# Backward queries kept in natural time order, and the two normed scan directions added on GpSimd, in a hybrid RWKV-7 / gMLP layer

## The chip, the cores and the metric

The kernel runs on one core of one Trainium2 chip. The metric is the time of one execution in microseconds of device time. Before the change it is 3197.58 us, the median of 3 runs (3194.99 to 3198.23).

## The reference, cut to what matters

One layer is computed over 640 tokens: 512 latent tokens (a grid of 64 columns) and 128 context tokens. Half of the mixing width goes through a bidirectional RWKV-7 scan with 16 heads of 64 channels, and it is the output of that scan that the change touches.

```python
def _delta_scan(r, w, k, v, aa, bb, s0, reverse):
    ...
    def step(S, inp):
        r_t, w_t, k_t, v_t, a_t, b_t = inp
        sa = jnp.einsum('bhvk,bhk->bhv', S, a_t)
        S = S * w_t[:, :, None, :] + sa[..., None] * b_t[:, :, None, :] + v_t[..., None] * k_t[:, :, None, :]
        return S, jnp.einsum('bhvk,bhk->bhv', S, r_t)
    s_fin, ys = lax.scan(step, s0, xs, reverse=reverse)
    return jnp.moveaxis(ys, 0, 1), s_fin

def _rwkv7_bidir(p, s0, lp):
    ...
    for d in range(2):
        ...
        y, s_fin = _delta_scan(rh, decay, kd, vh, -kk, kk * heads(a),
                               s0[:, d].astype(F32), reverse=(d == 1))
        out = out + _group_norm(y, lp['gn_w'], lp['gn_b']) \
            + jnp.sum(rh * kd * lp['r_k'], axis=-1, keepdims=True) * vh
        finals.append(s_fin)
    o = (out.reshape(B, T, D_A) * gate).astype(dtype)
```

The group norm runs over the 64 channels of a head, for each token and each direction by itself; the normed outputs of both directions are then added token by token. The rest of the layer (a gMLP half, the output projection, a SwiGLU block and RMS norms) is not touched.

## The kernel before, in words

All matrices are kept with channels on the partitions and the 640 tokens along the free axis. A *pair* is two heads, that is 128 channels; there are eight pairs. A *chunk* is 64 tokens; there are ten, eight latent and two context.

**First stage: per-pair preparation.** `take_k` (line 810) builds, for each pair and each direction `d`, a tile `R` with two halves per chunk: half 0 holds the scaled removal keys and half 1 the scaled queries (line 880). For the backward direction (`d == 1`) time runs backward inside a chunk; the helper `rev` (line 840) writes both halves with the 64 positions of a chunk reversed. `tail` (line 918) multiplies `X` and `R` chunk by chunk on TensorE into `pG`, and VectorE cuts the result with a triangular mask: columns 64 to 127, the query columns, go to `GR` (line 936). `R`, `GR` and the other factors are stored in the record `d_S` in device memory. The order of all instructions in this stage is planned by `Lister` (line 248), a planner that emits each instruction by a cost worked out from shapes alone (`Op`, line 104).

**Second stage: the recurrence.** `recur(p)` (line 1406) takes the chunks of a pair in order, both directions together. Its products on TensorE are `w_ps` (L1461), `u_ps` (L1476), `s_ps` (L1497) and the outputs `y_ps` (L1427, L1432), each with small steps on VectorE and ScalarE in between. ScalarE copies the outputs into `u.Y` (L1446), with tokens of a chunk on the partitions: 64 positions of head 0, then 64 positions of head 1, and channels along the free axis. For the backward direction the positions stand in reverse.

**The finish of a pair.** `finish(p)` (line 1511) normalises `u.Y` for each direction. GpSimd subtracts the mean (L1526), ScalarE squares (L1530), VectorE sums (L1531), GpSimd takes the inverse root (the helper `rsqrt`, L386) and multiplies by it (L1536), in two halves of five chunks each. TensorE then turns the result to channels on partitions and adds both directions on the way: for each chunk and head one product with the identity `I2` for the forward direction, and one with the reversed identity `J2` (line 1354) for the backward one, which undoes the reversal; both accumulate in the same PSUM tile `pO` (L1544). VectorE scales that into `bv` (L1548), the gate follows (`pG2`, L1562, L1563), and the result is stored to `d_o` (L1566).

```python
            for (a, b) in hv:
                ps = po.tile([P, 5, CH], F32, tag="g", name="pO")
                for cc in range(a, b):
                    for h in range(2):
                        for d in range(2):
                            TE.matmul(ps[hsl(h), cc - a, :], u.Y[hsl(h), d, cc, :], (J2 if d else I2)[hsl(h), :],
                                      start=(d == 0), stop=(d == 1))
```

**What orders the second stage.** A loop over hops (line 1603) advances up to two pairs of `recur`, and runs two mixers: `m2` holds the `finish` of the pair before, `m3` holds filler work, the part of the output projection that does not depend on the scan (`wout`, L1329 to L1331, and the turning of the input `pxT`, L1587). A mixer takes steps by a budget written into the `yield` statements. The engines' order within this stage is then set by the scheduler of the framework, from the program order and its own estimates; each engine's queue is fixed when the program is built, and an engine waits in order. After the loop, `finish` of the last pair runs with what is left of the filler work (lines 1617 to 1621), and the third stage, the other half of the output projection (L1736 to L1738), reads `d_o` back.

Of the kernel before, what the change touches and what calls it, by code (L numbers as in the profile page):

```python
# [10 lines left out]
F32 = mybir.dt.float32  # L11
# [3 lines left out]
ALU = mybir.AluOpType  # L15
# [4 lines left out]
P = 128  # L20
# [5 lines left out]
CH = 64  # L26
# [309 lines left out]
def flow_step(ctx: ExitStack, tc, x_prompt, x_sample, state_rwkv, c, c_ctx, w_mod, b_mod,  # L336
# [4 lines left out]
    V, S, G, TE = nc.vector, nc.scalar, nc.gpsimd, nc.tensor  # L341
# [21 lines left out]
    I2 = cb.tile([P, CH], F32, name="I2")  # L363
# [97 lines left out]
    with ExitStack() as ph:  # L461
# [38 lines left out]
        for t in range(NT):  # L500
            xt, c1 = xall[:, t, :], slice(t, t + 1)
# [139 lines left out]
    v3 = lambda ap: ap.rearrange("p (c t) -> p c t", t=CH)  # L641
# [7 lines left out]
    hsl = lambda h: slice(64 * h, 64 * h + 64)  # L649
# [160 lines left out]
    def take_k(pr, p, read):  # L810
# [28 lines left out]
        for d in range(2):  # L839
            rev = (lambda ap: ap[:, :, ::-1]) if d else (lambda ap: ap)  # L840
            last = 0 if d else CH - 1

            sg = bk.tile([P, T], F32, tag="t1", name="sg", bufs=2)
            tha = bp.tile([P, T], F32, tag="t3", name="tha", bufs=1)
            for hf in range(2):
                s = slice(HALF * hf, HALF * hf + HALF)
                for h, dst in enumerate((sg, tha)):
                    yield slots.free
                    ps = slots.tile([P, HALF], F32, "pwa")
                    yield lambda: (p, d) in wl  # L850
                    yield [oT.matmul(ps, w[:, h, :], waM[:, h, s], start=i == 0, stop=i == 1) for i, w in enumerate(wl[p, d])]
                    c = 16 * h + 8 * d + p
                    yield oS.activation(dst[:, s], ps, AF.Tanh, scale=0.5, bias=w0h[:, c:c + 1])
                    slots.done(ps)
            del wl[p, d]
            yield oS.activation(sg, sg, AF.Copy, scale=0.5, bias=0.5)
            L = bp.tile([P, T], F32, tag="t2", name="L", bufs=1)
            for lo in (0, HALF):
                s = slice(lo, lo + HALF)
                o_, i_ = (L[:, s][:, ::-1], sg[:, s][:, ::-1]) if d else (L[:, s], sg[:, s])  # L860
                yield oV.tensor_tensor_scan(out=o_, data0=scan1, data1=i_, initial=0.0, op0=ALU.mult, op1=ALU.add)
            gam = bk.tile([P, T], F32, tag="t1", name="gam", bufs=2)
            yield oS.activation(gam, L, AF.Exp, scale=-KAP)
            yield oS.activation(L, L, AF.Exp, scale=KAP)
            yield oS.copy(gend[:, p, d, :], v3(gam)[:, :, last])
            n3, g3, i3 = v3(nkk), v3(gam), v3(L)
            n = 2 * p + d
            yield lambda: gone["R"] == n
            R = bz.tile([P, NCH, 2, CH], F32, tag="R", name="R")
            ra = rev(R[:, :, 0, :])  # L870
            if d:
                yield oV.tensor_mul(ra[:, :, 0:CH - 1], n3[:, :, 0:CH - 1], g3[:, :, 1:CH])
                yield oS.copy(ra[:, :, CH - 1], n3[:, :, CH - 1])
            else:
                yield oV.tensor_mul(ra[:, :, 1:CH], n3[:, :, 1:CH], g3[:, :, 0:CH - 1])
                yield oS.copy(ra[:, :, 0], n3[:, :, 0])
            f = fs if d == 0 else bk.tile([P, T], F32, tag="t1", name="f", bufs=2)
            yield oS.activation(f, tha, AF.Identity, scale=kah[:, p:p + 1], bias=ka1[:, p:p + 1])
            zr = o.zr
            yield oV.tensor_mul(rev(R[:, :, 1, :]), v3(zr), g3)  # L880
            yield oQ.dma_start(d_S[p, :, d, :, F_R:F_R + P], R.rearrange("p c s t -> p c (s t)"))
            yield oV.scalar_tensor_tensor(out=tha, in0=tha, scalar=1.0, in1=nkk, op0=ALU.add, op1=ALU.mult)
            yield oV.tensor_mul(f, f, zk)

            yield lambda: gone["X"] == n
            X = bz.tile([P, NCH, 2, CH], F32, tag="X", name="X", bufs=1)
            yield oV.scalar_tensor_tensor(out=rev(X[:, :, 1, :]), in0=v3(tha), scalar=-0.5, in1=i3, op0=ALU.mult, op1=ALU.mult)
            yield oV.tensor_mul(rev(X[:, :, 0, :]), v3(f), i3)
            qT.append(tail(p, d, R, X))
            if d:  # L890
                yield oV.tensor_add(fs, fs, f)
# [26 lines left out]
    def tail(p, d, R, X):  # L918
# [6 lines left out]
        for (c0, c1) in ((0, 4), (4, 8), (8, NCH)):  # L925
            yield slots.pair
            two = [slots.tile([P, 4, P], F32, "pG") for h in range(2)]
            yield [oT.matmul(two[h][(osl if u else hsl)(h), cc - c0, :], X[hsl(h), cc, u, :],
                            R[hsl(h), cc, :, :].rearrange("p s t -> p (s t)"), start=True, stop=True)
                   for cc in range(c0, c1) for u in range(2) for h in (1, 0)]  # L930
            for h in range(2):
                s, q, ps = hsl(h), osl(h), two[h]
                mb = mask.unsqueeze(1).to_broadcast([P, c1 - c0, P])
                yield oS.copy(GB[q, c0:c1, :], ps[q, 0:c1 - c0, 0:CH])
                GR = bk.tile([P, 4, CH], F32, tag="GR", name="GR", bufs=2)
                yield oV.tensor_tensor(out=GR[:, 0:c1 - c0, :], in0=ps[:, 0:c1 - c0, CH:P], in1=mb[:, :, CH:P], op=ALU.mult)
                yield oV.tensor_tensor(out=GA[s, c0:c1, :], in0=ps[s, 0:c1 - c0, 0:CH], in1=mb[s, :, 0:CH], op=ALU.mult)
                slots.done(ps)
                yield oQ.dma_start(d_S[p, :, d, c0:c1, F_G + CH * h:F_G + CH * h + CH], GR[:, 0:c1 - c0, :])
# [405 lines left out]
    with ExitStack() as ph:  # L1345
# [4 lines left out]
        po = ph.enter_context(tc.tile_pool(name="po", bufs=1, space=PSUM))  # L1350
        py = ph.enter_context(tc.tile_pool(name="py", bufs=1, space=PSUM))

        J2 = sm.tile([P, CH], F32, name="J2", bufs=1)
        V.tensor_copy(J2, I2[:, ::-1])
        gh, gl, gq = (rw.tile([P, T], F32R, name=n) for n in ("gh", "gl", "gq"))
        nc.sync.dma_start(gl.bitcast(F32), d_gs[0:P])
        S.copy(gh, gl.bitcast(F32))
# [153 lines left out]
        def finish(p):  # L1511
# [9 lines left out]
            u = U[p]  # L1521
            for d in range(2):
# [11 lines left out]
                rsqrt(ys, ys)  # L1534
                for (a, b) in hv:
                    GNE.tensor_tensor(out=y[:, a:b], in0=y[:, a:b], in1=bc(ys[:, a:b], b - a), op=ALU.mult)  # L1536
                yield 2.0

            for (a, b) in hv:
                ps = po.tile([P, 5, CH], F32, tag="g", name="pO")  # L1540
                for cc in range(a, b):
                    for h in range(2):
                        for d in range(2):
                            TE.matmul(ps[hsl(h), cc - a, :], u.Y[hsl(h), d, cc, :], (J2 if d else I2)[hsl(h), :],  # L1544
                                      start=(d == 0), stop=(d == 1))
                    yield 0.4
                dst = v3(bv)[:, a:b, :]
                V.scalar_tensor_tensor(out=dst, in0=ps, scalar=prm[:, C_GW + p:C_GW + p + 1],  # L1548
                                       in1=dst, op0=ALU.mult, op1=ALU.add)
                yield 0.8  # L1550
# [736 lines left out]
```

## Time and profile before

| what | us |
|---|---|
| median of 3 runs | 3197.58 |
| the profiled execution: its own time | 3198.94 |
| its span, first to last instruction | 3197.2 |
| TensorE busy (matmul) | 3091.0 |
| VectorE busy | 2333.2 |
| ScalarE busy | 1450.4 |
| GpSimd busy | 1276.2 |
| first and last product into `pO` (L1544), from the start of the span | 1104.9 and 1336.7 |

Times in a timeline are counted from the start of the span. The recurrence and the finishes lie between about 1045 and 1341 us. A product of 32-bit operands appears in the trace as two matmul records and two weight loads, so the 320 products of L1544 (eight pairs, ten chunks, two heads, two directions) are 640 records. "64\*64" in a record means that the product uses a 64 by 64 part of the array, so that products of the two heads can run side by side. A matmul's own duration is longer than its share of the engine, because matmuls are pipelined: the spacing of starts says what one costs. "Idle before" names the idle time of an engine in front of an instruction, and what ended it.

### The profile page before, as it was taken

The page shows a single profiled execution, that of the slowest core. Times are in us where ns is not written, and L with a number is a line of the kernel's source. Part 1 is how long each engine was busy: PE and PEld are TensorE (multiplying, and loading weights), DVE is VectorE, ACT ScalarE, POOL GpSimd, SP SyncE. Part 2 cuts the span into 40 slices and gives each one's busy share as a digit, 9 for nine tenths or more (in the row PEclk, how much of TensorE's full clock was granted, in tenths as well). Part 3 has the DMA queues.
Part 4 walks back from the last instruction along what each step waited for, and adds up shares of the span by engine and source line. Part 5 has one row for each costly group of instructions (what it writes and reads, how often), then busy time and mean ns, then how long its engine had stood idle before and what let it go on. Part 6 is the DMA issues. An engine that isn't in the chain of part 4 may idle for free.

```text
span 3197.2 us, 73695 instructions
## 1 busy us (share of the span) xinstructions
PE 3091.0 (97%) x28892; PEld 2876.7 (90%) x28892; DVE 2333.2 (73%) x4104; ACT 1450.4 (45%) x3173; POOL 1276.2 (40%) x1138
## 2 busy tenths in 40 slices
PE   7999999999998999999899999999999999999996
PEld 4888888888878777889899999999999999999996
DVE  4567687776656667567887887877878777877787
ACT  4244555555533433246444444444444444444365
POOL 1001232322221132220456665666666644555543
PEclk9999999999999999999999999999999999999998
DMA  9768988889896677356343434334433354554453
GB/s 343 239 186 245 239 228 220 219 232 234 237 235 202 206 226 240 109 153 183 109 127 107 122 118 126 119 108 129 125 111 119 111 183 147 168 162 134 121 172 122
DMA packets 742331, 552.98 MB, mean 173 GB/s; under 512 B 142112, under 2 KB 678720, under 8 KB 733152
## 3 DMA queue, kind: packets, MB, share of 16 engines
q1 hardware_dynamic: 727280, 529.73, 56.1%
q0 software_dynamic: 12288, 17.95, 2.4%
q8 instruction: 227, 3.72, 0.5%
q14 instruction: 120, 0.98, 0.1%
q10 hardware_dynamic: 2416, 0.60, 0.1%
HBM read 438.74 MB, written 111.69 MB: 172 GB/s over the span
## 4 chain that ended last, share of the span: by engine, by line
PE 85%; DMA 5%; issue 4%; DVE 4%; ACT 1%; POOL 1%; SPq 0%; DVEq 0%; ACTq 0%; POOLq 0%
PE big L106 16%; PE P L1899 15%; PE P L1897 15%; PE P L1898 15%; DMA wt<-in_w_mod_dram 2%; PE pmod L106 2%; PE big L1329 2%; PE pG L106 1%; PE pblk L106 1%; PE big L1330 1%; PE big L1331 1%; PE y_ps L1432 1%; PE u_ps L1476 1%; DMA opd<-d_op 1%; DVE lo L1687 1%
## 5 line engine op out<-in xcount | busy, mean ns | idle before, releaser
L1899 PE MATMUL P<-xo,lo 128*128 128x320 f32 x2352 | 727.8, 310 | 7.4 <-DVE lo L1687 7.4
L1897 PE MATMUL P<-xo,hi 128*128 128x320 f32 x2352 | 728.0, 310 | 2.2 <-ACT hi L1686 2.2
L1898 PE MATMUL P<-xo,hi 128*128 128x320 f32 x2352 | 727.7, 309 | 0.0
L1687 DVE TENSOR_TENSOR lo<-raw,hi 128x512 fp32r<-128x512 f32 x532 | 517.2, 979 | 163.4 <-ACT hi L1686 161.3
L1686 ACT CAST hi<-raw 128x512 fp32r<-128x512 f32 x532 | 330.4, 622 | 505.4 <-PE P L1898 425.7
L1899 PEld LDWEIGHTS P<-xo,lo 128*128 128x128 f32 x2352 | 442.4, 188 | 7.9 <-DVE lo L1687 7.9
L1897 PEld LDWEIGHTS P<-xo,hi 128*128 128x128 f32 x2352 | 442.6, 188 | 2.4 <-ACT hi L1686 2.4
L1898 PEld LDWEIGHTS P<-xo,hi 128*128 128x128 f32 x2352 | 442.6, 188 | 0.0
L1797 POOL TENSOR_TENSOR raw<-raw 128x512 f32<-128x512 f32 x252 | 412.8, 1641 | 17.3 <-DVE lo L1687 4.1
L1897 PE MATMUL P<-xd,hi 128*128 128x320 f32 x1232 | 383.0, 311 | 7.2 <-ACT hi L1686 3.4
L106 PE MATMUL big<-h_hi,hi 128*128 128x320 f32 x1184 | 388.4, 328 | 0.7 <-DVE early L600 0.7
L1899 PE MATMUL P<-xd,lo 128*128 128x320 f32 x1232 | 383.2, 311 | 3.7 <-DVE lo L1687 3.6
L1898 PE MATMUL P<-xd,hi 128*128 128x320 f32 x1232 | 382.3, 310 | 0.1
L106 PE MATMUL big<-h_hi,lo 128*128 128x320 f32 x1184 | 365.2, 308 | 0.3 <-DVE lo L106 0.3
L106 PE MATMUL big<-h_lo,hi 128*128 128x320 f32 x1184 | 365.3, 308 | 0.0
L1797 POOL TENSOR_TENSOR t<-raw 128x512 f32<-128x512 f32 x84 | 133.3, 1587 | 460.5 <-DMA raw<-in_w_ffn_up_dram 348.2
L1686 ACT CAST hi<-rawd 128x512 fp32r<-128x512 f32 (+1 forms) x288 | 165.6, 585 | 225.6 <-PE P L1898 152.1
L106 PEld LDWEIGHTS big<-h_hi,hi 128*128 128x128 f32 x1184 | 223.3, 189 | 33.9 <-issue 28.8
L1687 DVE TENSOR_TENSOR lo<-rawd,hi 128x512 fp32r<-128x512 f32 (+1 forms) x288 | 218.8, 767 | 43.0 <-ACT hi L1686 39.3
L1897 PEld LDWEIGHTS P<-xd,hi 128*128 128x128 f32 x1232 | 232.7, 189 | 10.1 <-ACT P L2195 5.1
L1899 PEld LDWEIGHTS P<-xd,lo 128*128 128x128 f32 x1232 | 232.5, 189 | 6.2 <-DVE lo L1687 6.1
L1898 PEld LDWEIGHTS P<-xd,hi 128*128 128x128 f32 x1232 | 232.6, 189 | 0.5 <-DVE xd L1950 0.5
(408 smaller groups left out, 6423.5 us busy)
## 6 DMA issues: line engine op xcount, KB each, us to landing
wt<-in_w_mod_dram SPq DMA_DIRECT2D x96, 1024.0 KB
raw<-in_w_ffn_gate_dram SPq DMA_DIRECT2D x182, 256.0 KB
raw<-in_w_ffn_up_dram SPq DMA_DIRECT2D x182, 256.0 KB
rec<-d_S SPq DMA_DIRECT2D x80, 576.0 KB
raw<-in_w_in_dram SPq DMA_DIRECT2D x166, 256.0 KB
rawd<-in_w_ffn_down_dram SPq DMA_DIRECT2D x128, 256.0 KB
raw<-in_w_out_dram SPq DMA_DIRECT2D x96, 256.0 KB
xd<-d_os SPq DMA_DIRECT2D x66, 320.0 KB
```

Source lines behind the costliest of these rows:

```text
L106: self.eng, self.run = eng, lambda: fn(*args, **kw)
L1329: TE.matmul(halves[hf], hi[:, k, :], o_hi[kb][:, s], start=(k == 0), stop=False)
L1330: TE.matmul(halves[hf], hi[:, k, :], o_lo[kb][:, s], start=False, stop=False)
L1331: TE.matmul(halves[hf], lo[:, k, :], o_hi[kb][:, s], start=False, stop=(k == 3))
L1432: TE.matmul(ys[d][hsl(h), e, :], r[:, d, F_G + CH * h:F_G + CH * h + CH], r[:, d, F_Z + CH * h:F_Z + CH * h + CH], **kw)
L1476: TE.matmul(ups[q, d, :], r[q, d, F_T:F_T + CH], r[q, d, F_Z + CH * h:F_Z + CH * h + CH] if W is None else W[q, d, :], start=True, stop=True)
L1686: S.copy(hi[:, 0:nk], raw[:, 0:nk])
L1687: V.tensor_sub(lo[:, 0:nk], raw[:, 0:nk], hi[:, 0:nk].bitcast(F32))
L1797: G.tensor_tensor(out=o[:, 0:nk], in0=p[:, 0:nk], in1=q[:, 0:nk], op=ALU.subtract)
L1897: TE.matmul(ps, hi[:, k, :], xk[:, 0, :], start=f, stop=False)
L1898: TE.matmul(ps, hi[:, k, :], xk[:, 1, :], start=False, stop=False)
L1899: TE.matmul(ps, lo[:, k, :], xk[:, 0, :], start=False, stop=l)
```

## The change

The queries of the backward direction are written in natural order of time (no `rev` on the write at line 880), and the mask for their products is read in reverse instead (line 936). So the outputs of the backward direction come out of the recurrence in natural order too. In `finish`, after the multiply for the backward direction, GpSimd adds the forward direction's normed outputs into the backward tile, half by half. TensorE turns the sum with one product per chunk and head, by `I2`. The reversed identity `J2` is gone.

```diff
-            yield oV.tensor_mul(rev(R[:, :, 1, :]), v3(zr), g3)
+            yield oV.tensor_mul(R[:, :, 1, :], v3(zr), g3)
...
-                yield oV.tensor_tensor(out=GR[:, 0:c1 - c0, :], in0=ps[:, 0:c1 - c0, CH:P], in1=mb[:, :, CH:P], op=ALU.mult)
+                mq = mb[:, :, CH:P][:, :, ::-1] if d else mb[:, :, CH:P]
+                yield oV.tensor_tensor(out=GR[:, 0:c1 - c0, :], in0=ps[:, 0:c1 - c0, CH:P], in1=mq, op=ALU.mult)
...
-        J2 = sm.tile([P, CH], F32, name="J2", bufs=1)
-        V.tensor_copy(J2, I2[:, ::-1])
...
                 for (a, b) in hv:
                     GNE.tensor_tensor(out=y[:, a:b], in0=y[:, a:b], in1=bc(ys[:, a:b], b - a), op=ALU.mult)
+                    if d:
+                        GNE.tensor_tensor(out=y[:, a:b], in0=y[:, a:b], in1=u.Y[:, 0, a:b], op=ALU.add)
                 yield 2.0
...
                 for cc in range(a, b):
                     for h in range(2):
-                        for d in range(2):
-                            TE.matmul(ps[hsl(h), cc - a, :], u.Y[hsl(h), d, cc, :], (J2 if d else I2)[hsl(h), :],
-                                      start=(d == 0), stop=(d == 1))
+                        TE.matmul(ps[hsl(h), cc - a, :], u.Y[hsl(h), 1, cc, :], I2[hsl(h), :], start=True, stop=True)
```

## The prediction

> **What bounds the kernel now.** I read the page first, for the engine that the chain runs through, then the windows of the stage that the change touches.
>
> ```profile
> span 3197.2 us, 73695 instructions
> ...
> PE 85%; DMA 5%; issue 4%; DVE 4%; ACT 1%; POOL 1%; SPq 0%; DVEq 0%; ACTq 0%; POOLq 0%
> ```
> ```profile
> core 0: us, PE busy (x) PEld busy (x) DVE busy (x) ACT busy (x) POOL busy (x), PEclk, DMA share, GB/s
> ...
> 1210.00:1240.00 30.00, 30.00 (x462) 23.50 (x457) 19.71 (x65) 12.08 (x54) 10.46 (x14) 1.00 0.75 239
> ...
> 1300.00:1320.00 20.00, 18.92 (x247) 15.67 (x247) 10.73 (x30) 5.96 (x22) 6.17 (x9) 0.91 0.21 61
> ```
> ```profile
> 1322.00:1328.00 6.00, 0.69 (x8) 0.37 (x8) 1.38 (x4) 0.91 (x2) 5.67 (x7) 0.75 0.47 153
> 1328.00:1336.00 8.00, 8.00 (x69) 7.24 (x69) 1.74 (x3) 0.00 (x0) 0.44 (x1) 0.55 0.01 2
> ```
>
> The chain that ended last is 85% TensorE. In the middle of the recurrence TensorE is busy for 30.00 of 30 us; VectorE works 19.71 of them and GpSimd 10.46. So a product taken away there should be time saved, and work added to GpSimd has room. The end of the recurrence is another matter: from 1322 to 1328 TensorE works 0.69 of 6 us and GpSimd 5.67. There GpSimd sets the time, and after it TensorE runs for 8 us at a granted clock of 0.55.
>
> The waits say whom TensorE waits for in the recurrence (all of it, 1040 to 1345 us: total, times, longest), and the timeline where: three pairs out of eight.
>
> ```profile
> PE pO L1544 <- POOL Y L1536: 7.3, 5, 3.5
> ```
> ```profile
> 1164.44 0.33 PE L1544 MATMUL pO<-I,Y 64*64 64x64 f32 x2 [0.65 <-POOL Y L1536]
> ...
> 1168.31 0.27 PE L1544 MATMUL pO<-J,Y 64*64 64x64 f32 x1 [0.22 <-POOL Y L1536]
> ```
> ```profile
> 1302.61 0.27 PE L1544 MATMUL pO<-J,Y 64*64 64x64 f32 x1 [1.08 <-POOL Y L1536]
> ```
> ```profile
> 1324.01 0.33 PE L1544 MATMUL pO<-I,Y 64*64 64x64 f32 x2 [1.83 <-POOL Y L1536]
> 1327.82 0.36 PE L1544 MATMUL pO<-J,Y 64*64 64x64 f32 x1 [3.48 <-POOL Y L1536]
> ```
>
> These are the third, the seventh and the last pair. In the other five the products come well behind GpSimd. The smallest cover I found is that of the second pair:
>
> ```profile
> 1134.42 1.41 POOL L1536 TENSOR_TENSOR Y<-Y,ys 128x320 f32<-128x320 f32 x2
> ```
> ```profile
> 1137.92 0.34 PE L1544 MATMUL pO<-I,Y 64*64 64x64 f32 x4
> ```
>
> Its two multiplies start at 1134.42, the first half is ready 1.41/2 = 0.7 us later, and the first product starts at 1137.92, so 2.8 us are to spare.
>
> **The products removed.** Half of L1544 goes: 160 products, 320 matmul records.
>
> ```profile
> L1544 PE MATMUL pO<-J,Y 64*64 64x64 f32 x320 | 25.8, 226 | 4.8 <-POOL Y L1536 4.8
> ```
> ```profile
> 1335.84 0.33 PE L1544 MATMUL pO<-I,Y 64*64 64x64 f32 x4
> 1335.96 0.33 PE L1544 MATMUL pO<-J,Y 64*64 64x64 f32 x4
> ...
> 1336.66 0.33 PE L1544 MATMUL pO<-J,Y 64*64 64x64 f32 x4
> ```
> ```profile
> 1140.89 0.22 PE L1544 MATMUL pO<-I,Y 64*64 64x64 f32 x1
> ...
> 1141.42 0.39 PE L1427 MATMUL y_ps<-SN,rec 64*64 64x64 f32 x6
> ```
>
> The mean of 226 ns is latency; the spacing is the price. In a block of nothing but `pO`, seven groups of four take 1336.66 - 1335.84 = 0.82 us, 29 ns a record, and 320 records would be 9.4 us. Where the scheduler mixes `pO` with other 64 by 64 products that use the other corners of the array, 27 records start in 1141.42 - 1140.89 = 0.53 us, 20 ns each: 6.4 us. Most blocks in the timeline are pure, so I take 8.3 us, with 6.4 and 9.4 as ends. The twenty records of the last pair's first half run at the clock of 0.55, where each is 29/0.55 - 29 = 24 ns dearer: 0.5 us more. Together **-8.8 us** (-6.9 to -9.9). Nothing is late behind them: what follows `pO` on VectorE (L1548) waits for it, and comes earlier. The turns between 64 by 64 and full products stay, because the forward products stay.
>
> **The adds.** Two per pair, sixteen in all, on GpSimd: 128x320 with two full operands. The trace has no such add here; the multiplies of L1536 (1.41 us for two) read one full operand and a short one. Elsewhere GpSimd does it with two (min/median/max):
>
> ```profile
> L1656 POOL TENSOR_TENSOR x1T<-x1T,rs x16: 880/1114/1317, 1419.2 to 1435.3; 128x320 f32<-128x320 f32 x16
> ```
> ```profile
> L1997 POOL TENSOR_TENSOR s<-act x22: 861/1327/1389, 1549.5 to 2566.5; 128x320 f32<-128x320 f32 x22
> ```
>
> The bounds are 0.7 us (a multiply) and 1.3 (the median next to a busy VectorE). I take 0.9, near the least of both rows, since VectorE has a third of its time free here and almost none to do in the tail. GpSimd's own 16 x 0.9 = 14 us are covered. All that is queued behind the last multiply is the next pair's finish, which waits for ScalarE, 21 us in this pair:
>
> ```profile
> 1157.17 0.26 POOL L1524 TENSOR_SCALAR ys<-ys 128x10 f32<-128x10 f32 x1 [21.35 <-ACT Y L1446]
> ```
> ```profile
> 1327.04 1.40 POOL L1536 TENSOR_TENSOR Y<-Y,ys 128x320 f32<-128x320 f32 x2
> ```
> ```profile
> 1335.56 0.34 PE L1544 MATMUL pO<-I,Y 64*64 64x64 f32 x4
> ```
>
> Only the first product of a pair feels the add, 0.9 us later, because the order on GpSimd is multiply, add, multiply, add, and the second half's products come much later. In the tail they start at 1335.56, and the second add would end near 1327.04 + 2 x (0.7 + 0.9) = 1330.3.
>
> In five pairs 2.8 us and more cover 0.9. In the three others TensorE's queue stands: `u_ps`, `w_ps` and the filler behind `pO` wait with it. Seventh and last pair: +0.9 each. Third pair: the wait at 1168.31 becomes 0.22 + 0.9, but the forward product that waited 0.65 at 1164.44 goes, and so does the old 0.22: 1.12 - 0.87, about +0.2. Together **+2.0 us** (0 if other work slips in front; 3 x 1.3 = 3.9 at most).
>
> **The clock.** The window 1300 to 1320 has a granted clock of 0.91: 0.09 x 20 = 1.8 us lost, behind a wait of only 1.08 us. The new wait of some 1.1 us in the third pair is as long, and that of the seventh grows to 2. I count one more such loss: **+1.8 us** (0 to three, 5.4). The Trainium skill ("TensorE: Matmul & The Clock Gate", Part 1: The HAM clock gate) says that the array falls to half rate after at least one idle window of about 3.4 us. By that rule a wait of 1 to 2 us costs no clock and this term is 0; the row at 1300 speaks against it, as 1.08 us was enough there.
>
> **What costs nothing.** VectorE writes `R` forward instead of reversed and reads the mask reversed:
>
> ```profile
> L106 DVE TENSOR_TENSOR R<-zr,gam x16: 812/818/824, 223.8 to 851.1; 128x640 f32<-128x640 f32 x16
> ```
>
> Eight of these sixteen write in reverse and eight don't, and all lie between 812 and 824 ns: direction costs nothing. If the reversed read of a broadcast mask did cost, 48 instructions of `GR` would feel it, hidden under the wide products of the first stage. The planner's costs there go by shape, so that stage keeps its order, and its transfers keep their sizes. The copy into `J2` is one small VectorE instruction. The adds share memory with VectorE; how much that can hurt is seen where both are busy:
>
> ```profile
> L1687 DVE TENSOR_TENSOR lo<-raw,hi 128x512 fp32r<-128x512 f32 x532 | 517.2, 979 | 163.4 <-ACT hi L1686 161.3
> ```
> ```profile
> L1721 DVE TENSOR_TENSOR lo<-raw,hi 128x512 fp32r<-128x512 f32 x30 | 20.7, 690 | 19.6 <-ACT hi L1720 19.6
> ```
>
> 979 against 690 ns is a factor of 1.42; on 14 us of adds that is 6 us more of VectorE, which has 10 of every 30 us free. I count 0.
>
> **The sum** is -8.8 + 2.0 + 1.8 = -5.0 us. The profiled execution took 3198.94 us (1.7 more than its span) and would take 3193.9. It lies 1.4 us above the median of 3197.58, so the forecast median is **3192.6 us**. A difference under 0.2%, 6.4 us, is about what a measurement of this kernel cannot tell from none: the marks are 3191.2 and 3204.0.
>
> **Rivals.** (1) *No further loss of clock*: the longer waits cost only themselves, because a stretch of half clock needs more idle time than they make. For: the third pair's wait of 1.1 us stands alone. Against: the loss behind 1.08 us in the window from 1300. -8.8 + 2.0 = -6.8, 3190.8 us. This is how it goes by the rule of the Trainium skill cited above. (2) *The adds don't reach TensorE at all*: the scheduler's estimate now has `pO` ready later and puts filler in front, in all three places. These rows of the tail bear on it:
>
> ```profile
> 1321.87 0.31 PE L1331 MATMUL big<-oh,lo 128*128 128x320 f32 x1
> ```
> ```profile
> 1322.70 0.68 DVE L417 TENSOR_TENSOR lo<-raw,hi 128x512 fp32r<-128x512 f32 x1
> ```
>
> For: the weights of the next filler are split at 1323.4, before `pO` is ready. Against: the queue put a forward product right behind 1321.87 although its operand was 2 us off, so the scheduler takes GpSimd for faster than it is, and will again. -8.8, 3188.8 us. (3) *TensorE isn't the limit; the recurrence's own chain is* (`w_ps`, add, `u_ps`, copy, `s_ps`, add), and the products filled its gaps. What goes in seven pairs, 7 x 1.0 us, comes back as waits, and of the rest only the last pair's 1.0 + 0.5 remains, against its 0.9 for the add: about 0, 3197.6 us. Against it stands this row of the waits, in which VectorE waits for TensorE:
>
> ```profile
> DVE SN L1503 <- PE s_ps L1497: 21.2, 34, 1.6
> ```
>
> (4) *Slower*: with the backward product gone, one instruction now needs the whole chain of GpSimd, and the scheduler, which takes that chain for short, moves `pO` up in every pair to where it thinks it ready. Each pair then pays 0.9 for the add and 1.8 for the clock: 8 x 2.7 - 8.8 = +12.8, 3210.4 us. It passes the mark of 6.4 from (8.8 + 6.4)/2.7, six pairs on. Against it: five pairs have over 2.8 us of cover, set by the mixers' budgets, which stay as they are.
>
> **Chances.** The forecast 0.40, rival 1 0.27, rival 2 0.15, rival 3 0.10, rival 4 0.08. Faster by over 0.2% are rivals 1 and 2: 0.42. Slower is rival 4: 0.08. The rest is 0.50. The range goes from -9.9 with no wait and no clock (3187.7 us) to the dearest ends of the terms, -6.9 + 3.9 + 5.4 = +2.4 (3200.0 us); it leaves out rival 4 and little else.
>
> **What would show it.** Right: 320 records of L1544's product and no `J`; their spacing still near 29 ns; 16 adds on GpSimd near 0.9 us; TensorE's waits for `Y` up from 7.3 to about 9 us in the same three pairs; the first product of the last pair near 1 us later, counted from the end of GpSimd's last root; one more stretch at a clock near 0.5 between 1150 and 1320; the last product of the recurrence some 5 us earlier. Wrong: waits for `Y` in the other pairs (rival 4), none (rival 2), TensorE idle for VectorE within the hops (rival 3), adds over 1.3 us, or a time that moves outside the recurrence, in the first stage or behind 1345 us.

## The result and the profile after

The change makes the kernel slower by half a percent. The changed kernel takes 3213.86 us, the median of 4 runs (3211.51 to 3216.32); the kernel before takes 3196.32 us on the same chip (4 runs, 3194.99 to 3198.23). The ratio is 1.0052, with a 95% interval of 1.0038 to 1.0066. The forecast was 3192.6 us, and its range ended at 3200.0.

The profiled execution of the changed kernel took 3211.89 us. Most lines of the code stand one higher than before: the multiply is L1535, the add L1537, the products into `pO` L1544, the filler L1330 to L1332, the third stage from L1735.

The page after begins so:

```profile
span 3210.1 us, 73085 instructions
...
PE 3102.2 (97%) x28572; PEld 2880.3 (90%) x28572; DVE 2316.2 (72%) x4103; ACT 1453.8 (45%) x3173; POOL 1292.2 (40%) x1154
```

The 320 records are gone (28892 before, 28572 now), and yet TensorE is busy for longer: 3102.2 us against 3091.0. Fewer products that take more time point to the clock. To see in which stage, take the first product of the filler (it opens the second stage, that of the recurrence) and the first of the third stage. First the kernel before, then the changed one:

```profile
L1329 PE MATMUL big<-oh,hi x256: 302/412/636, 1000.7 to 1345.2; 128*128 128x320 f32 x128
```
```profile
L1736 PE MATMUL big<-oh,hi x256: 303/309/555, 1345.7 to 1480.3; 128*128 128x320 f32 x128
```
```profile
L1330 PE MATMUL big<-oh,hi x256: 302/412/636, 993.9 to 1354.3; 128*128 128x320 f32 x128
```
```profile
L1735 PE MATMUL big<-oh,hi x256: 304/309/935, 1354.8 to 1490.8; 128*128 128x320 f32 x128
```

The first stage ends 6.8 us earlier (1000.7 to 993.9), the second stage grows from 1345.7 - 1000.7 = 345.0 to 1354.8 - 993.9 = 360.9 us, so +15.9, and what lies behind it from 1851.5 to 1855.3, +3.8. Together that is the +12.9 us of the two spans. The first stage's 6.8 us are spread between executions: over all the profiles of this case it ends between 992.3 and 1000.7 us. What lies behind takes 1851.5 to 1853.6 us in the four profiles of kernels with both products and no add (the kernel before, e3, e8 and e9 below) and 1855.3 to 1860.9 in the ten others, so a few microseconds there may belong to the change; no run was made to show why. The main loss is in the second stage. The windows of it, before and after (us, TensorE busy, weight loads, VectorE, ScalarE, GpSimd, granted clock, DMA share, GB/s):

```profile
1040.00:1360.00 320.00, 311.87 (x4588) 252.63 (x4587) 208.18 (x654) 116.68 (x506) 85.66 (x112) 0.98 0.64 196
```
```profile
1040.00:1360.00 320.00, 308.67 (x4153) 243.03 (x4152) 199.84 (x636) 107.52 (x491) 99.09 (x128) 0.89 0.60 186
```

TensorE is idle 11.3 us instead of 8.1, a difference of only 3.2. But the clock falls from 0.98 to 0.89. Where it falls, in the changed kernel and then in the kernel before:

```profile
1150.00:1161.00 11.00, 9.24 (x156) 7.12 (x159) 6.79 (x23) 3.78 (x16) 9.59 (x12) 1.00 0.76 242
1161.00:1196.00 35.00, 35.00 (x329) 26.28 (x329) 15.64 (x51) 7.73 (x42) 3.31 (x6) 0.51 0.44 133
...
1300.00:1320.00 20.00, 17.00 (x161) 12.48 (x163) 8.28 (x25) 3.38 (x16) 6.19 (x8) 0.62 0.14 48
1320.00:1340.00 20.00, 13.78 (x101) 11.66 (x101) 8.15 (x20) 4.23 (x12) 12.47 (x16) 0.67 0.24 79
1340.00:1360.00 20.00, 20.00 (x141) 19.10 (x138) 11.04 (x23) 5.03 (x9) 0.10 (x1) 0.86 0.31 98
```
```profile
1161.00:1196.00 35.00, 33.95 (x553) 26.78 (x554) 25.37 (x85) 12.67 (x64) 14.03 (x18) 1.00 0.72 218
...
1320.00:1340.00 20.00, 14.69 (x134) 13.40 (x133) 7.34 (x17) 2.62 (x5) 7.95 (x9) 0.74 0.19 63
```

From 1161 to 1196 TensorE looks perfectly busy, 35.00 of 35 us, and gets 329 records done where it did 553 before. Only the clock column tells why. Busy time times lost clock is 35.00 x 0.49 + 17.00 x 0.38 + 13.78 x 0.33 + 20.00 x 0.14 = 31.0 us after, and 18.92 x 0.09 + 14.69 x 0.26 = 5.5 us before: 25.5 us more. It is an upper bound, since a product held up by its operand loses less than half of its time to the clock.

The waits for `Y` and the three places in the timeline:

```profile
PE pO L1544 <- POOL Y L1537: 11.0, 3, 6.2
```
```profile
1160.02 0.56 PE L1544 MATMUL pO<-I,Y 64*64 64x64 f32 x10 [1.76 <-POOL Y L1537]
```
```profile
1305.88 0.58 PE L1544 MATMUL pO<-I,Y 64*64 64x64 f32 x5 [3.00 <-POOL Y L1537]
```
```profile
1339.34 1.33 PE L1544 MATMUL pO<-I,Y 64*64 64x64 f32 x20 [6.22 <-POOL Y L1537]
```

They are the third pair, the seventh and the last, as before. But before the change forward products stood between the waits of the third pair (0.65 and 0.22 us) and of the last (1.83 and 3.48); the seventh had one wait of 1.08 us. Now each pair has one wait, of 1.76, 3.00 and 6.22 us. The half clock starts 1.35 us behind the end of the first, at 1161.37, and 1.85 us into the second, at 1304.73 (rows below, under the rule weighed in the prediction).

GpSimd in the third pair:

```profile
1157.75 1.40 POOL L1535 TENSOR_TENSOR Y<-Y,ys 128x320 f32<-128x320 f32 x2
1159.11 1.67 POOL L1537 TENSOR_TENSOR Y<-Y 128x320 f32<-128x320 f32 x2
```
```profile
L1537 POOL TENSOR_TENSOR Y<-Y x16: 854/859/1312, 1095.8 to 1339.2; 128x320 f32<-128x320 f32 x16
```

Both multiplies come first and both adds behind them, so the first half is ready one multiply (0.7 us) later than the code reads.

### The profile page after: what moved, and what is told of

Read it like the earlier page. It is cut to its first block, busy times and chain, and to the rows that moved or that the text cites. A ratio compares the mean times of both kernels' runs of the same rounds, so it can differ in the third digit from the quotient of the medians.

```text
span 3210.1 us, 73085 instructions
## 1 busy us (share of the span) xinstructions
PE 3102.2 (97%) x28572; PEld 2880.3 (90%) x28572; DVE 2316.2 (72%) x4103; ACT 1453.8 (45%) x3173; POOL 1292.2 (40%) x1154
## 5 line engine op out<-in xcount | busy, mean ns | idle before, releaser
L1686 DVE TENSOR_TENSOR lo<-raw,hi 128x512 fp32r<-128x512 f32 x532 | 499.6, 946 | 182.2 <-ACT hi L1685 180.6
L1896 PEld LDWEIGHTS P<-xd,hi 128*128 128x128 f32 x1232 | 232.5, 189 | 10.2 <-ACT P L2194 6.1
```

The lines of the kernel that those rows point to most:

```text
L1686: V.tensor_sub(lo[:, 0:nk], raw[:, 0:nk], hi[:, 0:nk].bitcast(F32))
L1896: TE.matmul(ps, hi[:, k, :], xk[:, 0, :], start=f, stop=False)
```

## The experiments

**Theory A, the clock.** The products saved are saved. But the forward products used to cut TensorE's wait for GpSimd; one longer wait lets the clock fall to half, and under the small products of the recurrence it stays there for tens of microseconds. **Rival B**: the adds, or the waits for them, cost by themselves. **Rival C**: the new order of the queues costs, whatever the waits. **Rival D**: chance. The letters are those of the last eight expectations. In the first four theory A and rival C mean the same, but rival B is another thought, which the first of them spells out. Ratios are against the kernel before on the same chip, with 95% intervals. Each run's result lists its mean granted clock; 87 runs of the kernel before lie between 0.985 and 0.990.

**e1, no add.** The changed kernel without the add; the forward direction is missing from its output.

```diff
-                    if d:
-                        GNE.tensor_tensor(out=y[:, a:b], in0=y[:, a:b], in1=u.Y[:, 0, a:b], op=ALU.add)
```

> The changed kernel without the adds: GpSimd does the work of before, TensorE turns the backward direction alone, so the forward direction is left out of the output. Theory A (the loss is the clock: TensorE waits for the add in the third and the seventh pair, and the half clock that follows lasts 34 and 24 us): without the add the wait in the third pair shrinks from 1.8 us to under 1, no long stretch of half clock follows, and the time is some 8 us below before, near 3188. Rival B (the products taken away were not the limit; what comes back is latency of the recurrence): the time is within 3 us of before, near 3196. Rival C (the new order of the queues is slower by itself): well above before, near 3205 or more.

3200.87 us, ratio 1.0017 (0.9994 to 1.0041), in two groups: six runs between 3191.0 and 3201.8 us at clocks of 0.985 to 0.989, and four between 3212.4 and 3218.6 us at 0.978 to 0.980. Its waits in the profile, and the place where the clock fell (in that execution not in the third pair):

```profile
PE pO L1542 <- POOL Y L1535: 9.9, 3, 5.9
```
```profile
1164.44 0.33 PE L1542 MATMUL pO<-I,Y 64*64 64x64 f32 x4 [1.60 <-POOL Y L1535]
```
```profile
1150.00:1200.00 50.00, 48.39 (x730) 37.09 (x729) 34.04 (x114) 17.78 (x84) 21.22 (x28) 1.00 0.76 223
1290.00:1325.00 35.00, 28.89 (x270) 22.33 (x270) 18.18 (x50) 8.72 (x32) 15.46 (x21) 0.79 0.24 79
```

No add, and still waits of 1.60 us and more, and a group of runs at a low clock. All three expectations missed, theory A's by its wait (under 1 us) as well as its time (near 3188). Taking the forward products out of the queue is enough to make the long waits.

**e2, the add and both products.** The add stays, and the two products per chunk and head come back, both by `I2` (the forward direction is counted twice in the output).

```diff
-                        TE.matmul(ps[hsl(h), cc - a, :], u.Y[hsl(h), 1, cc, :], I2[hsl(h), :], start=True, stop=True)
+                        for d in range(2):
+                            TE.matmul(ps[hsl(h), cc - a, :], u.Y[hsl(h), d, cc, :], I2[hsl(h), :],
+                                      start=(d == 0), stop=(d == 1))
```

> The changed kernel with the adds, but with both products of before, forward and backward, into the same sum: the forward direction counts twice in the output. This is the add alone, without the gain. Theory A: the wait for the add is there in the last pair and where the products stand close behind GpSimd; if a long stretch of half clock follows in the recurrence, the time is above that of the changed kernel, 3215 to 3225; if none follows, 3 to 5 us above before. In both cases the time goes with the total of half clock between 1030 and 1350 us. Rival B: 2 to 4 us above before, whatever the clock. Rival C: as the changed kernel, near 3214.

3202.89 us, ratio 1.0014 (1.0001 to 1.0028). It does all that the changed kernel does and 160 products more, and is 11 us faster than it, which speaks against rival C. The add together with the waits that it makes costs 3.8 us by the medians, 9 at most by the interval. Theory A without a long stretch and rival B both allowed that, so this run doesn't part them. Its third pair waits 0.65 and 0.43 us, with the clock at 1.00; the other two pairs:

```profile
1300.70 0.48 PE L1545 MATMUL pO<-I,Y 64*64 64x64 f32 x4 [2.58 <-POOL Y L1537]
1324.33 0.33 PE L1545 MATMUL pO<-I,Y 64*64 64x64 f32 x2 [1.84 <-POOL Y L1535]
1329.64 2.40 PE L1545 MATMUL pO<-I,Y 64*64 64x64 f32 x38 [4.35 <-POOL Y L1537]
```

**e3, natural order alone.** The kernel before with the queries in natural order and both products by `I2`, no add.

```diff
-            yield oV.tensor_mul(rev(R[:, :, 1, :]), v3(zr), g3)
+            yield oV.tensor_mul(R[:, :, 1, :], v3(zr), g3)
...
-                            TE.matmul(ps[hsl(h), cc - a, :], u.Y[hsl(h), d, cc, :], (J2 if d else I2)[hsl(h), :],
+                            TE.matmul(ps[hsl(h), cc - a, :], u.Y[hsl(h), d, cc, :], I2[hsl(h), :],
```

> Only the first part of the change: backward queries in natural order, mask read in reverse, both products by the same identity, no add. Computes the reference. Theory A and rival B: the same as before within 3 us, with the waits and the clock of before (one short stretch of 3.4 us behind the seventh pair and 10 us in the tail). Rival C, or a price of the mask read in reverse: the time is 8 us or more above before, and in the second case the groups that write GR are longer than 416 ns.

3200.46 us, ratio 1.0005 (0.9993 to 1.0016), with waits of 7.3 us as before the change. The first half of the change, which the prediction costed at nothing, costs nothing that can be measured.

**e4, the add on VectorE.**

```diff
-                        GNE.tensor_tensor(out=y[:, a:b], in0=y[:, a:b], in1=u.Y[:, 0, a:b], op=ALU.add)
+                        V.tensor_tensor(out=y[:, a:b], in0=y[:, a:b], in1=u.Y[:, 0, a:b], op=ALU.add)
```

> The changed kernel with the sixteen adds on VectorE instead of GpSimd. Computes the reference. Theory A: an add there is some 0.5 us instead of 0.84 and need not stand behind the second multiply, so the wait in the third pair falls from 1.8 to about 1 us and the long stretches of half clock shorten or go: 3190 to 3200. If the wait stays over 1.5 us the long stretch stays too, and so does the time. Rival B: near 3214, as VectorE's chain now carries 8 us more. Rival C: near 3214.

3204.61 us, ratio 1.0025 (1.0008 to 1.0043); two runs of ten have a low clock (3214.8 and 3223.9 us, at 0.981 and 0.979). A faster add (633 ns by the median) shortens the waits (the seventh pair's to 1.37 us, the third's to 1.30) and brings back half of the loss, less than theory A expected (3190 to 3200 us). The runs at a low clock remain.

```profile
1301.71 0.68 PE L1544 MATMUL pO<-I,Y 64*64 64x64 f32 x16 [1.37 <-DVE Y L1537]
```
```profile
1290.00:1325.00 35.00, 29.11 (x320) 22.51 (x318) 22.95 (x58) 11.29 (x40) 19.35 (x25) 1.00 0.28 88
```

In the profiled execution no half clock follows these two waits. It follows another one, in the second pair, where TensorE waits for ScalarE (`s_ps`, L1496). Neither an add nor `Y` is what TensorE waits for there, and yet 15 x 0.34 / 0.5 = 10.2 us of half clock come with 1.50 us of waiting:

```profile
1133.12 0.45 PE L1496 MATMUL s_ps<-rec 128*64 128x64 f32 x8 [1.50 <-ACT rec L1479]
```
```profile
1130.00:1145.00 15.00, 13.50 (x169) 10.77 (x168) 8.22 (x27) 2.92 (x17) 2.15 (x3) 0.66 0.38 123
```

**e5, the changed kernel again**, unaltered.

> The changed kernel unaltered, ten more runs on the chip of the three below. Theory A (the loss is clock: the products saved are saved, but the wait that the forward product used to split is now one wait, the clock falls to half behind it and stays there for 20 to 35 us of small products): every run near a mean clock of 0.98 and between 3209 and 3219 us, with 50 us or more of half clock between 1150 and 1350 us of its profile. Rival D (it was a chance phase of the four runs so far): at least a third of the runs at a clock of 0.986 or more and 3190 to 3198 us. Rival B (the wait for the adds costs by itself, no clock needed): 3210 to 3217 us at any clock.

3214.84 us (5 runs), ratio 1.0048 (1.0032 to 1.0064): four at clocks of 0.979 and 0.980, one at 0.983 and 3205.9 us. With the first four runs that makes nine of nine at 0.983 or less, against none of 87 for the kernel before. Rival D falls. The stretch in the third pair is there again:

```profile
1150.00:1200.00 50.00, 48.24 (x532) 36.43 (x531) 25.80 (x86) 13.90 (x67) 15.32 (x22) 0.66 0.53 162
```

**e6, products later.** A line in front of the products into `pO`; no work is added or removed.

```diff
                 yield 2.0
 
+            yield 6.0
             for (a, b) in hv:
                 ps = po.tile([P, 5, CH], F32, tag="g", name="pO")
```

> The change, with the products into pO put later in the program (a budget of 6 more in front of them), so that the adds are done when TensorE comes to them. Theory A: the waits of pO for GpSimd's Y go from 11.0 to under 5 us, the half clock of the recurrence from 68 to under 20 us, the mean clock to 0.986 or more, and the time to 3192 to 3199 us, 15 or more below the changed kernel. Rival B: the time falls by the waits that go, 6 us, to 3206 to 3210 us. Rival C (the new order of the queues costs, whatever the waits): it stays within 5 us of the changed kernel.

3190.18 us (9 runs), ratio 0.9976 (0.9966 to 0.9986). This version beats both kernels: 24.7 us below the changed kernel measured with it, where rival B allowed 6, and faster than the kernel before. It is also 1.8 us below the range of theory A; e9 shows one reason. All runs lie at 0.988 to 0.990. One wait is left, in the last pair:

```profile
PE pO L1544 <- POOL Y L1537: 3.8, 1, 3.8
```
```profile
1150.00:1200.00 50.00, 50.00 (x792) 39.06 (x794) 36.59 (x122) 18.95 (x90) 25.50 (x32) 1.00 0.75 233
1290.00:1325.00 35.00, 30.83 (x326) 25.55 (x323) 19.62 (x51) 9.00 (x30) 19.20 (x21) 0.95 0.30 93
```

From 1150 to 1200 TensorE gets 792 records done where the changed kernel (e5, above) did 532.

**e7, the wait split again.** One forward product per pair is put back in front, under 1 us in all; the backward product behind it overwrites what it wrote.

```diff
-                ps = po.tile([P, 5, CH], F32, tag="g", name="pO")
+                ps = po.tile([P, 5, CH], F32, tag="g", name="pO"); a == 0 and TE.matmul(ps[hsl(0), 0, :], u.Y[hsl(0), 0, 0, :], I2[hsl(0), :], start=True, stop=True)
```

> The change with one forward product put back in front of the products of each pair (chunk 0, head 0; what it writes is overwritten by the product behind it). Nothing else returns: 16 more matmul records in all, under 1 us. It doesn't wait for the add, so TensorE's wait is cut in two pieces as before the change. Theory A: the mean clock goes to 0.985 or more in most runs, half clock in the recurrence under 35 us, 3194 to 3203 us. Rivals B and C: no change, 3210 to 3218 us.

3204.59 us, ratio 1.0019 (1.0007 to 1.0032), clocks of 0.982 to 0.986. That is 10.3 us faster than the changed kernel measured with it, with work added: rivals B and C expected no change. It stays 1.6 us above what theory A expected, and four of ten runs reach the clock of 0.985 that it expected of most. The profile shows where. The new product splits the wait in the third pair (L1541 is the product put back) and in the last one; in the seventh the wait is still 3.01 us in one piece, and there the clock still falls.

```profile
1162.35 0.32 PE L1541 MATMUL pO<-I,Y 64*64 64x64 f32 x2 [0.52 <-POOL Y L1535]
1168.01 0.44 PE L1544 MATMUL pO<-I,Y 64*64 64x64 f32 x6 [0.68 <-POOL Y L1537]
```
```profile
1299.55 0.58 PE L1544 MATMUL pO<-I,Y 64*64 64x64 f32 x5 [3.01 <-POOL Y L1537]
```
```profile
1150.00:1200.00 50.00, 48.52 (x751) 37.52 (x750) 35.03 (x117) 17.95 (x85) 24.46 (x32) 1.00 0.74 229
1290.00:1325.00 35.00, 31.99 (x266) 24.39 (x263) 15.67 (x44) 8.05 (x33) 12.54 (x18) 0.66 0.16 50
```

**e8, a longer wait in the kernel before.** Six steps more on GpSimd in the third pair.

```diff
-                rsqrt(ys, ys)
+                rsqrt(ys, ys); [G.tensor_scalar(ys, ys, 1.0, None, op0=ALU.mult) for _ in range(6 if d and p == 2 else 0)]
```

> The kernel before, with six small steps more on GpSimd (128x10) in the finish of the third pair only, about 1.5 us in front of the multiply of the backward direction: products, adds and first stage as before, one wait longer. Theory A: a stretch of half clock of 10 us or more behind the third pair's wait (near 1165 us) in the profile or in some of the runs, whose clock then is 0.982 to 0.985 and whose time is 6 to 18 us above the kernel before. Rival B: plus 1.5 us at most, at an unchanged clock. If the queue has moved other work in front and the wait isn't longer, it says nothing.

3198.43 us, ratio 1.0001 (0.9991 to 1.0010). The steps took 2.01 us, but other work slipped in front and the wait only grew from 0.22 to 0.97 us; the clock stayed at 1.00. It tells theory A and rival B apart no further; it shows that a wait of just under 1 us beside one of 0.65 cost no clock in ten runs (0.987 to 0.990).

```profile
1169.89 0.27 PE L1544 MATMUL pO<-J,Y 64*64 64x64 f32 x1 [0.97 <-POOL Y L1536]
```

**e9, the kernel before with its products later**, by the same line as in e6.

> The kernel before with its products into pO put later by the same budget of 6, both directions turned by products, no add. It tells what of the gain of the kernel with the later products comes from the place and what from the change. If the 160 products saved are worth their spacing (8.8 us) and the adds are covered except in the last pair (about 1 us), it is 6 to 9 us slower than that kernel: 3196 to 3199 us. If the products only filled gaps (the third rival of the prediction), both are within 2 us: 3188 to 3192 us. If the place matters most, it is also 3 to 8 us faster than the kernel before.

3193.81 us, ratio 0.9990 (0.9981 to 0.9999). It falls between the first two expectations; the third, a gain of 3 to 8 us by the place, holds with 4.3 by the medians (0.3 to 6 by the interval). TensorE's products have then no wait for `Y` left at all, where e6 and e12 keep one in the last pair; what the change is worth is read together with e12, below.

**e10, products later in the third pair alone.**

```diff
+            yield 6.0 * (p == 2)
             for (a, b) in hv:
```

> The changed kernel with the products later in the third pair alone. Its wait of 1.76 us goes, the seventh pair and the last keep theirs (3.0 and 6.2). Theory A: the 34 us of half clock from 1161 go with it, which is 17 us of work, so 3194 to 3200 us at a clock of 0.984 or more, with half clock of 20 us or more left behind the seventh pair. Rival B (waits cost themselves): 3211 to 3213 us. Rival C (order of the queues): any, but the third pair's window without a loss of clock and no gain would speak for it.

3202.50 us, ratio 1.0006 (0.9995 to 1.0017), no run below 0.984. The third pair's stretch is gone, the seventh pair's is there behind a wait of 3.01 us (20.5 us). The time is 2.5 us above what theory A expected, and 8.5 below the least that rival B allowed.

```profile
1150.00:1200.00 50.00, 50.00 (x742) 38.38 (x741) 35.05 (x117) 18.41 (x89) 25.04 (x32) 1.00 0.75 221
1290.00:1325.00 35.00, 31.16 (x265) 24.24 (x263) 17.72 (x47) 7.76 (x29) 14.94 (x19) 0.71 0.18 53
```

**e11, GpSimd's order held.** Multiplies and adds stay in the order of the program, which the prediction had assumed. TensorE's order is that of the changed kernel but for a few rows of the seventh pair.

```diff
+            u = U[p]; K = lambda i: tc.keep_in_program_order(i)
...
-                    GNE.tensor_tensor(out=y[:, a:b], in0=y[:, a:b], in1=bc(ys[:, a:b], b - a), op=ALU.mult)
+                    K(GNE.tensor_tensor(out=y[:, a:b], in0=y[:, a:b], in1=bc(ys[:, a:b], b - a), op=ALU.mult))
                     if d:
-                        GNE.tensor_tensor(out=y[:, a:b], in0=y[:, a:b], in1=u.Y[:, 0, a:b], op=ALU.add)
+                        K(GNE.tensor_tensor(out=y[:, a:b], in0=y[:, a:b], in1=u.Y[:, 0, a:b], op=ALU.add))
```

> The changed kernel with GpSimd's multiplies and adds held in the order of the program (multiply, add, multiply, add), which is the order that the prediction took; TensorE's order is the same up to a few rows in the seventh pair. Each first product waits one multiply less, 0.7 us: the third pair's 1.76 us becomes about 1.1, the seventh's 3.0 about 2.3, the last one's 6.2 about 5.5. If the clock falls behind any wait of a microsecond, the half clock stays at 50 us or more and the time at 3209 to 3216 us. If 1.1 us is too short for it, the 34 us in the third pair go, and the time is 3194 to 3203 us. If the prediction's waits were right and only the order was wrong, 3191 to 3196 us.

3201.58 us, ratio 1.0019 (0.9999 to 1.0039), again in groups: four of ten runs at 0.983 or less (3205.6, and 3216.1 to 3219.9 us), six between 3194.4 and 3202.7 us. The waits in the profile:

```profile
1162.44 0.56 PE L1544 MATMUL pO<-I,Y 64*64 64x64 f32 x10 [1.21 <-POOL Y L1537]
```
```profile
1294.20 0.58 PE L1544 MATMUL pO<-I,Y 64*64 64x64 f32 x5 [2.82 <-POOL Y L1537]
```

A third pair that waits 1.21 us instead of 1.76, with TensorE's order there untouched, takes the runs at a low clock from nine of nine to four of ten. So TensorE's new order there isn't enough for the loss; what changed in that pair is GpSimd's order and with it the wait.

**e12, products later and GpSimd's order held.**

> The change with the products later and GpSimd's order held, both together. TensorE's order is that of the kernel with the products later. Only the last pair waits there (3.8 us), and it would wait about 3.1: 0.5 to 1 us faster than that kernel, 3188 to 3191 us, at the same clock of 0.989. If the clock is what matters and no wait is left to set it off in the other pairs, it can't be slower.

3189.62 us, ratio 0.9975 (0.9962 to 0.9989), clocks of 0.987 to 0.990: as fast as e6 within what can be told. Against e9 it is the change itself, with the waits out of the middle of the recurrence in both. TensorE's busy time on the two pages, e9 and then e12:

```profile
PE 3091.6 (97%) x28892; PEld 2874.2 (90%) x28892; DVE 2319.6 (73%) x4104; ACT 1449.7 (45%) x3173; POOL 1273.8 (40%) x1138
```
```profile
PE 3082.4 (97%) x28572; PEld 2863.5 (90%) x28572; DVE 2327.8 (73%) x4103; ACT 1449.4 (46%) x3173; POOL 1291.6 (41%) x1154
```

At the same clock in both profiled executions (0.989), 320 records fewer are 3091.6 - 3082.4 = 9.2 us of TensorE (6.3 by the page of e6, with 3085.3). Of this the wait that the last pair keeps takes back a third:

```profile
1315.19 0.45 PE L1544 MATMUL pO<-I,Y 64*64 64x64 f32 x8 [3.25 <-POOL Y L1537]
```

9.2 - 3.25 leaves 6; the medians differ by 4.2 us, with intervals of 3 us (e9) and 4 us (e12) on either side, so the times alone don't rule out none. The second stage says more: by the rows used for the result it takes 338.3 us in e9, 335.1 in e6 and 331.9 in e12.

**The runs side by side.** The waits for `Y` in two pairs, by the profile, and how many runs had a clock of 0.983 or less:

| kernel | third pair's waits, us | seventh pair's wait, us | runs at 0.983 or less |
|---|---|---|---|
| changed kernel (first runs and e5) | 1.76 | 3.00 | 9 of 9 |
| e1 | 1.60 | 2.39 | 4 of 10 |
| e4 | 1.30 | 1.37 | 2 of 10 |
| e11 | 1.21 | 2.82 | 4 of 10 |
| e8 | 0.65, 0.97 | 1.07 | 0 of 10 |
| e2 | 0.65, 0.43 | 2.58 | 1 of 10 |
| e7 | 0.52, 0.68 | 3.01 | 4 of 10 (0.982 and 0.983) |
| before; e3 | 0.65, 0.22 | 1.08 | 0 of 87; 0 of 10 |
| e10 | none | 3.01 | 0 of 10 |
| e6, e9, e12 | none | none | 0 of 29 |

A run's clock doesn't say in which pair it was lost. Runs at 0.980 or less are found only where the third pair waits 1.21 us or more: five of nine, four, one and three of ten. e7 and e10, with the seventh pair's wait whole, stay at 0.982 or more.

The profiles part the wait from the clock. Half clock is the time at a granted clock of 0.50 between 1040 and 1360 us:

| profile | second stage, us | waits for `Y`, us | half clock, us |
|---|---|---|---|
| e12 | 331.9 | 3.3 | 3.4 |
| e6 | 335.1 | 3.8 | 3.4 |
| e11 | 345.3 | 9.9 | 30.7 |
| e10 | 347.6 | 9.0 | 27.3 |
| e7 | 350.5 | 10.0 | 34.1 |
| changed kernel | 360.9 | 11.0 | 68.3 |
| e5 | 362.0 | 10.8 | 64.9 |

e11 waits almost as long as the changed kernel and its second stage is 15.6 us shorter, with 37.6 us less of half clock. That is against rival B.

## Why the prediction was wrong

**What held.** The bound was read rightly: TensorE sets the time in the recurrence. The products removed were forecast at -8.8 us (-6.9 to -9.9); TensorE's busy time falls by 9.2 us from e9 to e12 and by 6.3 from e9 to e6. The adds were taken as 0.9 us and cost 0.84 (1.67 us for two in the third pair, a median of 0.859 over all). The three pairs that wait were named rightly, and no other pair began to wait. Natural order of time costs nothing that can be measured (e3). GpSimd has room, and VectorE did not get slower.

**The step that failed** is the clock: "I count one more such loss: +1.8 us (0 to three, 5.4)." The loss grew by up to 25 us, from 5.5 to 31.0 by the windows. Its mechanism was named, a wait behind which the clock falls, and the new stretch at half clock that it expected between 1150 and 1320 came; the size was wrong, and with it the sign of the sum. The term carried the length of a loss over from the one row at hand, the 1.8 us behind 1300. That is a stretch of 3.41 us at half clock, the shortest in any profile here. The same term with measured stretches is 17.2 us for the third pair alone. The fences of the prediction already held a warning, which it used only for the price of twenty records: from 1328 to 1336 the clock was 0.55 for 8 us while TensorE was busy for 8.00.

**A smaller step that failed too** is the wait itself. The forecast for the third pair was 1.12 us, with GpSimd's order as multiply, add, multiply, add. The scheduler put both multiplies first, and the wait was 1.76. With the order held (e11) it was 1.21, near the forecast, and six of ten runs were then at 3194.4 to 3202.7 us. In the seventh pair the forecast was 2, and the wait was 3.00, and 2.82 with the order held. There TensorE comes to its products earlier against GpSimd: 0.73 us before the backward multiply starts (1.11 in e11), where it was 0.30 us before the change. The waits together were forecast to rise from 7.3 to about 9 us, and rose to 11.0; held in order, they make 1.21 + 2.82 + 5.83 = 9.9, the last one from the list of waits, whose longest is 5.8.

**The rivals.** Rival 1 (waits cost only themselves) and rival 2 (adds never reach TensorE) fall with the clock; e6 and e12 show what rival 2 would have looked like, 3190 us against its 3188.8, though e9 puts part of that down to the place. Rival 3 falls by the profiles: e12's second stage is 6.4 us shorter than e9's, and TensorE's only new wait there of over half a microsecond is that of the last pair; the run times alone would leave it open. Rival 4 had the right sign and a near result, 3210.4 us, for another reason, by luck: it spread a loss of 1.8 us over eight pairs, and in truth two pairs lose the clock for 34.13 and 23.89 us (the rows below).

**The rule weighed in the prediction.** The trace shows the clock fall behind 1.76 us of idle time, and then, window by window:

```profile
1157.95:1161.37 3.42, 1.66 (x48) 1.32 (x44) 1.32 (x6) 0.26 (x1) 2.83 (x4) 1.00 1.01 368
1161.37:1195.50 34.13, 34.13 (x310) 25.52 (x311) 15.28 (x50) 7.73 (x42) 3.31 (x6) 0.50 0.44 133
...
1304.73:1328.62 23.89, 22.74 (x175) 17.22 (x176) 8.76 (x24) 4.24 (x19) 3.58 (x6) 0.50 0.11 31
1335.45:1345.69 10.24, 6.35 (x39) 6.18 (x39) 1.16 (x3) 0.41 (x1) 4.57 (x5) 0.50 0.07 22
```

TensorE worked 1.66 of the 3.42 us ahead of the fall, and its longest idle time there was 1.76 us. And 34.13 us of unbroken busy time did not bring the clock back. The Trainium skill ("TensorE: Matmul & The Clock Gate", Part 1: The HAM clock gate) gives half rate after at least one idle window of about 3.4 us and the full rate after at least one busy window of that length. Read with the profile's busy time, neither half holds for this trace of small products, and the measurement decides; the prediction was right to set the rule aside for the fall and did not ask what it would mean for the return. The same section of the Trainium skill says that the window is free-running. That would fit the groups of runs in e1 and e11 (the same wait falls into one window or across two), but no run here was made to show it.

**What stays open.** Why the stretch is 34 us in the third pair, 20 to 24 us in the seventh (e10, e11, e7 and the changed kernel) and 10.24 us near the end was not tried. The stretches are 10, 7 and 3 times 3.413 us, so a loss comes in steps here. In e6 the last pair's wait of 3.81 us is followed by only 35 x 0.05 / 0.5 = 3.5 us, so the length of the wait alone doesn't set it. That the small products hold the clock down, and the wide ones of the filler let it return sooner, is argued from these places alone.

## What to carry to other kernels

Price a wait on TensorE by the clock behind it too, and take the length of the loss from the same mix of products: here 1.76 us of waiting cost 17 us of work by the windows, and taking that wait away (e10) brought back some 13 us by the two ratios. Before removing instructions from a queue, look at what stands between its waits: one forward product per pair, put back, brought 10.3 us (e7), more than the 9 us of time that all the forward products take. And when a product gets a later operand, move its place in the queue as well; that one line turned a loss of 0.5% into a gain of 0.24%, of which the kernel before gets 0.1% from the same line (e9).

## What the runs showed of the hardware

The busy share hides a halved clock completely: 35.00 of 35 us busy, at 0.51, with 329 records instead of 553. In the seventh pair the half clock that followed was longer behind longer waits, though not strictly: none behind 1.07 and 1.37 us (e8, e4), 3.4 us behind 1.08 (before, e3), 13.7 and 10.2 behind 2.39 and 2.58 (e1, e2), and 20.5 to 23.9 behind 2.82 to 3.01 (e11, e10, e7 and both profiles of the changed kernel). A wait for ScalarE did the same: 10.2 us followed 1.50 us of it (e4). The mean granted clock of a run says more than its time: one kernel, unaltered between its runs, gave 3191.0 us at 0.989 and 3218.6 us at 0.979 (e1).
